# First two projections with K outermost and both token tiles inside, in a hybrid decoder trunk on one core

## The chip, the cores and the metric

One core of one Trainium2 chip. The time is the device time of one execution in microseconds (us). TensorE, VectorE (DVE), ScalarE (ACT), GpSimd (POOL) and SyncE (SP, which issues all transfers here) each run their own queue in order. In the rows PE is TensorE's matmuls and PEld its weight loads.

## What is computed

Two layers on a sequence of 256 tokens and 1024 features, all in float32. Each layer is `x + RMSNorm(mixer(RMSNorm(x)))`; layer 0 is gated linear attention (GLA), layer 1 sparse attention. The change lies in the first projections of layer 0.

```python
def gla_mixer(h, w_in, w_gk_up, b_gk, head_norm, w_out):
    p = (h @ w_in).astype(jnp.float32)
    q, k, v, glr, z = jnp.split(p, [GLA_QK, 2 * GLA_QK, 2 * GLA_QK + GLA_V,
                                    2 * GLA_QK + GLA_V + GLA_GATE_RANK], axis=-1)
    gk = jax.nn.log_sigmoid(glr @ w_gk_up + b_gk) / GLA_GATE_NORMALIZER
    ...
    return o @ w_out
```

## The kernel before

The tokens are two tiles of 128 rows. `h` is x times the norm's gain, transposed so that K (the 1024 features, 8 blocks of 128) lies on the partitions; the row's reciprocal RMS is multiplied in later, when a projection leaves PSUM. Float32 products are kept exact enough by splitting each operand into a rounded high half (`hi`) and the rest (`lo`); a product is three matmuls, hi·hi, and hi·lo and lo·hi (`mm3`, lines 200 to 203). ScalarE writes the high half (a copy that rounds: line 180 for weights, 300 for h); VectorE or POOL subtracts it to get the low half (lines 186 and 301). Which of the two does it is the table `LOS`, one tuple per weight chunk; listed blocks go to POOL.

Weights come in chunks of up to 512 columns (`Chunk`), loaded as four units of two K blocks through four raw buffers (`N_RAW`). A raw buffer is free for the next load when both blocks of its unit are split. All transfers go through one queue on SP in source order (`dma`).

The start of the program, lines 365 to 400: `ch_r` is the first chunk, 352 columns (called r here: the last third of v and the gate's low rank part), then `ch_k` (512 columns, k) and `ch_q` (q). x's first tile comes in two halves of K, its second in one transfer behind all of r's weights. `warm` issues matmuls on a tile of ones. `pre_T` transposes four K blocks of a tile on TensorE, multiplies by the gain (line 297), and splits (300, 301). `proj` (line 212) runs one tile through all eight K blocks, 24 matmuls, then the other tile. `rms` takes two squares with sums on ScalarE (line 315), then VectorE and POOL make the reciprocal root. Rotary angles for layer 1 are made on VectorE (lines 404 to 417: one cast and eight short passes, most on 128x64), their sine and cosine on ScalarE (421 to 424), and behind the cosine ScalarE loads another activation table (428). `spread` (line 320) puts the reciprocal RMS of both tiles on a row with two matmuls (line 329).

What sets the order: the build's scheduler places each engine's instructions, except where `after` or `chain` ties one to the one before it in the source; `act` does so for some of ScalarE's.

Of the kernel before, what the change touches and what calls it, by code (L numbers as in the profile page):

```python
# [23 lines left out]
LOS = ((0, 1, 5, 6, 7), (0, 3, 4, 7), (3, 5, 6), (0, 1, 2, 3, 4, 5, 7), (0, 2, 4, 5, 6), (2, 3, 5, 7), (0, 2, 3, 5, 6), (3, 5, 7), (3, 4, 5, 7), (3, 5, 6), (4, 5, 6, 7), (1, 2, 4, 5, 7), (5, 6), (0, 2, 3, 5), (2, 5, 6), (2, 3, 5, 6, 7), (0, 2, 4, 6), (0, 1, 2, 3, 4, 5, 6, 7), (1, 2, 5))  # L24
# [5 lines left out]
WARM = (7, 1, 7)  # L30
# [57 lines left out]
def hybrid_kernel(ctx: ExitStack, tc: tile.TileContext, x, positions, pre_norm, post_norm,  # L88
# [67 lines left out]
    dma(grow, pre_norm.rearrange("l (k p) -> (l k) p", p=P))  # L156

# [239 lines left out]
    rs0[0], act[0] = rms(0, act[0])  # L397
    for c in range(2):
        act[0] = pre_T(1, c, 0, hT, "s", act[0])
    rs0[1], act[0] = rms(1, act[0])  # L400
# [9 lines left out]
    nc.vector.tensor_scalar(kr, ang, float(1.0 / (2 * np.pi)), MAGIC, op0=ALU.mult, op1=ALU.add)  # L410
    nc.vector.tensor_scalar(kr, kr, MAGIC, None, op0=ALU.subtract)
# [9 lines left out]
    act[0] = after(nc.scalar.activation(SNt[:, :, 1, :], ang, AF.Sin), act[0])  # L421
    nc.scalar.activation(kr, ang, AF.Abs)
    nc.vector.tensor_scalar(kr, kr, -1.0, float(np.pi / 2), op0=ALU.mult, op1=ALU.add)
    sin = nc.scalar.activation(CSt[:, :, 0, :], kr, AF.Sin)
    nc.vector.tensor_scalar(SNt[:, :, 0, :], SNt[:, :, 1, :], -1.0, None, op0=ALU.mult)
    nc.vector.tensor_copy(CSt[:, :, 1, :], CSt[:, :, 0, :])
    with tc.issue_after(sin.ins):
        nc.scalar.preload_act_table_set("natural_log_exp_and_others")
# [7 lines left out]
    ch_k = Chunk(w_in, G_K, 512).load()  # L436
    dma(C1, cst[:, C_L0:C_L1])
# [675 lines left out]
```

## Time and profile before

| | us |
|---|---|
| median of 3 runs (lowest, highest) | 304.49 (303.96, 304.69) |
| profiled execution | 304.3 |
| its span | 302.5 |
| TensorE busy | 285.9 (94%) |
| VectorE, ScalarE, POOL busy | 218.3, 179.2, 164.0 |

The span is the stretch from the first to the last instruction of the profiled execution; its own time lies 1.8 us above it. A busy TensorE means that matmuls were in flight; how dense they were is seen from the distance between their starts. All times in rows are counted from the span's start.

### The profile page before, as it was taken

The page shows a single profiled execution, that of the slowest core. Times are in us where ns is not written, and L with a number is a line of the kernel's source. Part 1 is how long each engine was busy: PE and PEld are TensorE (multiplying, and loading weights), DVE is VectorE, ACT ScalarE, POOL GpSimd, SP SyncE. Part 2 cuts the span into 40 slices and gives each one's busy share as a digit, 9 for nine tenths or more (in the row PEclk, how much of TensorE's full clock was granted, in tenths as well). Part 3 has the DMA queues.
Part 4 walks back from the last instruction along what each step waited for, and adds up shares of the span by engine and source line. Part 5 has one row for each costly group of instructions (what it writes and reads, how often), then busy time and mean ns, then how long its engine had stood idle before and what let it go on. Part 6 is the DMA issues. An engine that isn't in the chain of part 4 may idle for free.

```text
span 302.5 us, 5366 instructions
## 1 busy us (share of the span) xinstructions
PE 285.9 (94%) x1800; PEld 240.1 (79%) x1800; DVE 218.3 (72%) x547; ACT 179.2 (59%) x456; POOL 164.0 (54%) x185
## 2 busy tenths in 40 slices
PE   6998999999999999999979999999899899999991
PEld 6975899999999788777868766899688678677561
DVE  1999628876787758896795544879997999696423
ACT  3697668776595245844533434649896668475311
POOL 2664945898247206473728133598749956424300
PEclk9799999999999999999999999999999999999999
DMA  6976662882847406368583855777404400010001
GB/s 195 314 246 200 185 192 69 275 263 63 307 113 231 144 3 164 117 140 284 149 250 97 259 174 198 272 209 214 136 2 139 142 1 0 2 70 0 2 0 69
DMA packets 28156, 44.56 MB, mean 147 GB/s; under 512 B 2849, under 2 KB 12497, under 8 KB 28130
## 3 DMA queue, kind: packets, MB, share of 16 engines
q1 hardware_dynamic: 28130, 44.23, 47.8%
q8 instruction: 14, 0.23, 0.3%
q14 instruction: 12, 0.10, 0.1%
HBM read 43.18 MB, written 1.05 MB: 146 GB/s over the span
## 4 chain that ended last, share of the span: by engine, by line
PE 54%; DVE 21%; issue 8%; ACT 7%; DMA 6%; POOL 3%; SPq 1%; DVEq 0%; POOLq 0%; ACTq 0%
PE acc L201 10%; PE acc L203 9%; PE acc L202 9%; DVE lo L186 6%; PE o L946 3%; ACT hi L180 3%; PE s L202 3%; PE s L203 3%; PE s L201 3%; PE o L752 3%; DMA raw<-in_gla_w_in_dram 3%; PE s L859 3%; PE t L932 3%; DMA x_sb<-in_x_dram 2%; DMA raw<-in_nsa_w_out_dram 1%
## 5 line engine op out<-in xcount | busy, mean ns | idle before, releaser
L186 POOL TENSOR_TENSOR lo<-raw,hi 128x512 fp32r<-128x512 f32 (+3 forms) x81 | 102.5, 1287 | 58.9 <-ACT hi L180 52.1
L180 ACT ACTIVATE hi<-raw 128x512 fp32r<-128x512 f32 (+3 forms) x152 | 80.3, 580 | 38.4 <-DMA raw<-in_nsa_w_in_dram 23.6
L186 DVE TENSOR_TENSOR lo<-raw,hi 128x512 fp32r<-128x512 f32 (+3 forms) x71 | 61.4, 890 | 17.2 <-ACT hi L180 17.1
L203 PE MATMUL acc<-hi,hT 128*128 128x512 f32 (+3 forms) x128 | 44.6, 349 | 1.0 <-DVE hT L301 1.0
L201 PE MATMUL acc<-hT,hi 128*128 128x256 f32 x160 | 45.3, 284 | 0.1
L203 PE MATMUL acc<-hT,lo 128*128 128x256 f32 x160 | 45.0, 282 | 0.0
L202 PE MATMUL acc<-hT,hi 128*128 128x256 f32 x160 | 44.6, 279 | 0.0
L201 PE MATMUL acc<-hi,hT 128*128 128x512 f32 (+3 forms) x128 | 44.6, 348 | 0.0
L202 PE MATMUL acc<-lo,hT 128*128 128x512 f32 (+3 forms) x128 | 44.2, 346 | 0.0
L903 POOL TENSOR_SCALAR P<-P,cf 128x128 f32<-128x128 f32 (+1 forms) x64 | 30.0, 487 | 26.0 <-DVE cf L899 14.0
L866 ACT ACTIVATE P<-P,mn 128x128 f32<-128x128 f32 (+1 forms) x64 | 28.4, 445 | 9.0 <-DVE mn L864 5.1
L203 PEld LDWEIGHTS acc<-hT,lo 128*128 128x128 f32 x160 | 30.0, 188 | 0.4 <-issue 0.4
L201 PEld LDWEIGHTS acc<-hT,hi 128*128 128x128 f32 x160 | 30.0, 188 | 0.4 <-DVE z L355 0.3
L202 PEld LDWEIGHTS acc<-hT,hi 128*128 128x128 f32 x160 | 30.1, 188 | 0.2
L203 PEld LDWEIGHTS acc<-hi,hT 128*128 128x128 f32 x128 | 24.2, 189 | 4.7 <-DVE hT L301 2.4
L201 PEld LDWEIGHTS acc<-hi,hT 128*128 128x128 f32 x128 | 24.3, 190 | 3.1 <-ACT hi L180 0.4
L202 PEld LDWEIGHTS acc<-lo,hT 128*128 128x128 f32 x128 | 24.4, 190 | 2.1
L864 DVE CUSTOM_DVE_ANT_0 P<-s,c 128x128 f32<-128x128 f32 (+1 forms) x64 | 20.8, 348 | 4.9 <-PE s L859 3.7
L932 PE MATMUL t<-c,P 128*128 128x128 f32 x96 | 16.6, 284 | 0.4 <-DVE qS L827 0.4
L265 POOL TENSOR_TENSOR ss<-ss,cols 128x1 f32<-128x1 f32 x4 | 2.2, 554 | 25.7 <-DVE ss L264 25.7
L932 PEld LDWEIGHTS t<-c,P 128*128 128x128 f32 x96 | 10.6, 141 | 6.2 <-issue 3.8
L690 POOL TENSOR_TENSOR dup<-rt,rt 128x512 f32<-128x512 f32 x6 | 8.6, 1433 | 11.1 <-DVE rt L683 9.0
(235 smaller groups left out, 623.5 us busy)
## 6 DMA issues: line engine op xcount, KB each, us to landing
raw<-in_nsa_w_in_dram SPq DMA_DIRECT2D x24, 512.0 KB, 4.4
raw<-in_gla_w_in_dram SPq DMA_DIRECT2D x16, 512.0 KB, 4.6
raw<-in_gla_w_out_dram SPq DMA_DIRECT2D x8, 512.0 KB, 4.3
raw<-in_nsa_w_out_dram SPq DMA_DIRECT2D x8, 512.0 KB, 4.4
raw<-in_gla_w_in_dram SPq DMA_DIRECT2D x8, 344.0 KB, 3.6
raw<-in_nsa_w_in_dram SPq DMA_DIRECT2D x8, 280.0 KB, 3.2
w<-in_nsa_ck_w_dram SPq DMA_DIRECT2D x4, 512.0 KB, 4.0
w<-in_nsa_cv_w_dram SPq DMA_DIRECT2D x4, 512.0 KB, 4.7
```

The source lines that it names most:

```text
L180: m = after(nc.scalar.activation(hi[:, j, :n], raw[:, j, :n], AF.Copy), prev)
L186: eng.tensor_sub(lo[:, j, :n], raw[:, j, :n], f(hi[:, j, :n]))
L201: m = nc.tensor.matmul(o, a[0], b[0], start=start, stop=False, **kw)
L202: nc.tensor.matmul(o, a[0], b[1], start=False, stop=False, **kw)
L203: return m, nc.tensor.matmul(o, a[1], b[0], start=False, stop=stop, **kw)
L752: nc.tensor.matmul(hid_b[kv * 64:(kv + 1) * 64, :CHID], flat[:, j, kv].rearrange("p g c -> p (g c)"), w1[u * 2 + kv][:, j % 4, :], start=( ...
L859: pe(nc.tensor.matmul(o, q[i], k[:, g, c0:c1], start=(m == 0), stop=(m == 1)))
L864: nc.vector.tensor_tensor_reduce(out=o, in0=src, in1=masks[br], op0=ALU.add, op1=ALU.min, scale=-0.125, scalar=3.0e38, accum_out=self.mn[: ...
L866: nc.scalar.activation(o, o, AF.Exp, scale=-1.0, bias=self.mn[:, j:j + 1], accum_out=self.sm[:, j:j + 1])
L903: nc.gpsimd.tensor_scalar(o, o, cf[:, i * 2 + br:i * 2 + br + 1], 1.0, op0=ALU.mult, op1=ALU.mult)
L932: pe(nc.tensor.transpose(b[:, i * P:(i + 1) * P], self.Pt[i][:, c0:c0 + P], ident))
L946: pe(nc.tensor.matmul(ob[a * 64:(a + 1) * 64, :], (vs_sb, vw_sb)[br][:, kt, g * DH:(g + 1) * DH], pv[:, a], start=(br == y == 0), stop=Fal ...
```

## The change

`ch_r` and `ch_k` no longer go through `proj`. A new function `both` takes one K block and issues six matmuls, the three products for tile 0 and tile 1 in turn, into two PSUM banks; K is the outer loop. h's blocks are made in the order tile 0 first half, tile 1 first half, tile 0 second half, tile 1 second half; the transposes of the second half stand between the matmuls of K blocks 1, 2 and 3. To feed this, x's second tile comes in two halves: its first ahead of r's weights, the second halves of both tiles between the second and the third unit of r's weights. `line` ties the instructions of VectorE, ScalarE and POOL in these steps to source order (`line("dve", ...)` and so on), `in_order` those of TensorE. The squares of tile 0 (`rms(0)`) now stand between the absolute value and the cosine, those of tile 1 between k's first and second unit. The splits of r's low halves are dealt out otherwise (first tuple of `LOS`), and there are 11 instead of 15 warm-up matmuls. The results of r leave PSUM after k's matmuls.

```diff
-LOS = ((0, 1, 5, 6, 7), (0, 3, 4, 7), ...
+LOS = ((0, 2, 3, 5, 6), (0, 3, 4, 7), ...
-WARM = (7, 1, 7)
+WARM = (7, 4)
...
     dma(grow, pre_norm.rearrange("l (k p) -> (l k) p", p=P))
+    dma(X[:, 1, :H], xv[:, 1, :H])
...
-    ch_r = Chunk(w_in, 1712, 352).load(0, 2)
-    dma(X[:, 0, H:], xv[:, 0, H:])
-    ch_r.load(2, 8)
-    dma(X[:, 1, :], xv[:, 1, :])
+    ch_r = Chunk(w_in, 1712, 352).load(0, 4)
+    for t in range(NT):
+        dma(X[:, t, H:], xv[:, t, H:])
+    ch_r.load(4, 8)
...
+    def line(e, ins):
+        queues[e] = after(ins, queues.get(e))
+        return ins
+
+    def in_order(ins):
+        after(ins, last[0])
+        last[0] = ins
...
+    def first_T(t, c):
+        b = bank("ts"[c])
+        for k in range(4):
+            in_order(nc.tensor.transpose(b[:, k * P:(k + 1) * P], X[:, t, (c * 4 + k) * P:(c * 4 + k + 1) * P], ident))
+        xg = base.tile([P, 4, P], F32, tag="xg", name=nm("xg"), bufs=2)
+        def rest():
+            line("dve", nc.vector.tensor_tensor(xg, b.rearrange("p (k n) -> p k n", k=4),
+                                                gT[:, c * 4:c * 4 + 4].unsqueeze(2).to_broadcast([P, 4, P]),
+                                                op=ALU.mult))
+            hi, lo = (a[:, c * 4:c * 4 + 4, t * P:(t + 1) * P] for a in hT)
+            line("act", nc.scalar.activation(hi, xg, AF.Copy))
+            line("dve", nc.vector.tensor_sub(lo, xg, f(hi)))
+        return rest
+
+    def split_in_line(chunk, u):
+        n, raw = chunk.n, chunk.raw[u]
+        hi, lo = (wp.tile([P, 2, 512], F32R, tag=a, name=nm(a), bufs=N_HI) for a in ("hi", "lo"))
+        for j in range(2):
+            line("act", nc.scalar.activation(hi[:, j, :n], raw[:, j, :n], AF.Copy))
+            e, eng = ("pool", nc.gpsimd) if u * 2 + j in chunk.pool else ("dve", nc.vector)
+            line(e, eng.tensor_sub(lo[:, j, :n], raw[:, j, :n], f(hi[:, j, :n])))
+        chunk.u.append((hi, lo))
+
+    def both(o, chunk, k):
+        w = chunk.part(k)
+        for i, j in ((0, 0), (1, 0), (0, 1)):
+            for t in range(NT):
+                m = nc.tensor.matmul(o[t][:, :chunk.n], hT[i][:, k, t * P:(t + 1) * P], w[j], start=(k == i == j == 0),
+                                     stop=(k == KT - 1 and j == 1))
+                in_order(m)
+                chunk.mm.setdefault(2 * k + t, m)
...
-    act[0] = pre_T(0, 0, 0, hT, "t", act[0])
-    act[0] = ch_r.split_unit(act[0])
-    warm(WARM[1])
-    act[0] = pre_T(0, 1, 0, hT, "t", act[0])
-    warm(WARM[2])
-    for u in range(1, 4):
-        act[0] = ch_r.split_unit(act[0])
+    rest.append(first_T(1, 0))
+    for go in rest:
+        go()
+    warm(WARM[1])
+    o_r = [bank("acc") for _ in range(NT)]
+    split_in_line(ch_r, 0)
+    both(o_r, ch_r, 0)
+    split_in_line(ch_r, 1)
+    both(o_r, ch_r, 1)
+    for t in range(NT):
+        first_T(t, 1)()
+        both(o_r, ch_r, 2 + t)
+    for u in (2, 3):
+        split_in_line(ch_r, u)
+        for k in (2 * u, 2 * u + 1):
+            both(o_r, ch_r, k)
...
+    def tables():
+        line("act", nc.scalar.activation(SNt[:, :, 1, :], ang, AF.Sin))
+        line("act", nc.scalar.activation(kr, ang, AF.Abs))
+        nc.vector.tensor_scalar(kr, kr, -1.0, float(np.pi / 2), op0=ALU.mult, op1=ALU.add)
+        rs0[0], queues["act"] = rms(0, queues["act"])
+        sin = line("act", nc.scalar.activation(CSt[:, :, 0, :], kr, AF.Sin))
...
+        with tc.issue_after(sin.ins):
+            queues["act"] = nc.scalar.preload_act_table_set("natural_log_exp_and_others") or sin
+
+    tables()
...
     ch_k = Chunk(w_in, G_K, 512).load()
+    for t in range(NT):
+        if t == 1:
+            rs0[1], queues["act"] = rms(1, queues["act"])
+        split_in_line(ch_k, t)
...
+    o_k = [bank("s") for _ in range(NT)]
+    for u in range(4):
+        if u > 1:
+            split_in_line(ch_k, u)
+        for k in (2 * u, 2 * u + 1):
+            both(o_k, ch_k, k)
```

What this makes of the queues is shown at three places. The first is TensorE where r starts, before: `o` are the warm-up matmuls on `ones`, `t` transposes of x, `acc_240` the bank of tile 0, `hi_117` and `lo_118` the weights of K blocks 0 and 1, `hT_95` and `hT_96` h's high and low half.

```order
L379 MATMUL o_97<-ones 128x128
L292 MATMUL t_124<-c_64,x_sb 128x128 x4
L379 MATMUL o_97<-ones 128x128 x7
L201 MATMUL acc_240<-hi_117,hT_95 128x352
L202 MATMUL acc_240<-lo_118,hT_95 128x352
L203 MATMUL acc_240<-hi_117,hT_96 128x352
```

The same place in the changed program (line numbers are its own; `acc_131` and `acc_132` are the banks of tile 0 and tile 1, `hT_96` and `hT_97` the halves of h):

```order
L395 MATMUL t_115<-c_64,x_sb 128x128 x4
L389 MATMUL o_98<-ones 128x128 x4
L422 MATMUL acc_131<-hi_133,hT_96 128x352
L422 MATMUL acc_132<-hi_133,hT_96 128x352
L422 MATMUL acc_131<-hi_133,hT_97 128x352
L422 MATMUL acc_132<-hi_133,hT_97 128x352
L422 MATMUL acc_131<-lo_134,hT_96 128x352
L422 MATMUL acc_132<-lo_134,hT_96 128x352
```

The two tiles alternate, and the weights' low half is used last of the three.

The second is ScalarE from r's last weights (`hi_152`) to k's first units (`hi_314`, `hi_320`, `hi_326`), before; `junk` are the squares, `hT_95` rounds h of the second tile:

```order
L180 ACTIVATE hi_152<-raw_90 128x352 x2
L315 ACTIVATE junk_159,ss_158<-x_sb 128x512
L315 ACTIVATE junk_161,ss_158<-x_sb 128x512
L300 ACTIVATE hT_95<-xg_173 128x4x128
L180 ACTIVATE hi_314<-raw_221 128x512 x2
L300 ACTIVATE hT_95<-xg_182 128x4x128
L315 ACTIVATE junk_187,ss_186<-x_sb 128x512
L180 ACTIVATE hi_320<-raw_223 128x512 x2
L315 ACTIVATE junk_189,ss_186<-x_sb 128x512
L180 ACTIVATE hi_326<-raw_225 128x512 x2
L421 ACTIVATE sin_t<-ang 128x2x32
L422 ACTIVATE kr<-ang 128x64
```

The same stretch in the changed program (`hi_187`, `hi_205` are r's last two units, `hi_266` and `hi_282` k's first two):

```order
L412 ACTIVATE hi_187<-raw_90 128x352 x2
L412 ACTIVATE hi_205<-raw_92 128x352 x2
L472 ACTIVATE sin_t<-ang 128x2x32
L473 ACTIVATE kr<-ang 128x64
L316 ACTIVATE junk_240,ss_239<-x_sb 128x512
L316 ACTIVATE junk_242,ss_239<-x_sb 128x512
L476 ACTIVATE cos_t<-kr 128x2x32
L480 ACT_TABLE_LOAD
L412 ACTIVATE hi_266<-raw_258 128x512 x2
L316 ACTIVATE junk_273,ss_272<-x_sb 128x512
L316 ACTIVATE junk_275,ss_272<-x_sb 128x512
L412 ACTIVATE hi_282<-raw_260 128x512 x2
```

The sine, the cosine and the table load moved ahead of k's first unit; the squares of tile 0 moved behind the sine.

The third is VectorE in the same stretch, before: `lo_141` and `lo_147` are low halves of r's weights, `xg` products of the second tile, `ang` and `kr` the angles.

```order
L186 TENSOR_TENSOR lo_141<-raw_86,hi_140 128x352 x2
L186 TENSOR_TENSOR lo_147<-raw_88,hi_146 128x352
L404 CAST cols<-posi 128x2
L408 TENSOR_SCALAR ang<-c_64,cols 128x32 x2
L297 TENSOR_TENSOR xg_173<-s_168,gT 128x512
L410 TENSOR_SCALAR kr<-ang 128x64
L297 TENSOR_TENSOR xg_182<-s_177,gT 128x512
L411 TENSOR_SCALAR kr<-kr 128x64
L316 TENSOR_TENSOR ss_158<-ss_158 128x1
L301 TENSOR_TENSOR hT_96<-xg_173,hT_95 128x4x128
```

In the changed program (`xg_162` and `xg_177` are the second halves of K of tile 0 and 1, `lo_188` and `lo_206` the low halves of r's last units that fall to VectorE):

```order
L399 TENSOR_TENSOR xg_162<-s_157,gT 128x512
L404 TENSOR_TENSOR hT_97<-xg_162,hT_96 128x4x128
L399 TENSOR_TENSOR xg_177<-s_172,gT 128x512
L404 TENSOR_TENSOR hT_97<-xg_177,hT_96 128x4x128
L414 TENSOR_TENSOR lo_188<-raw_90,hi_187 128x352
L414 TENSOR_TENSOR lo_206<-raw_92,hi_205 128x352
L455 CAST cols<-posi 128x2
L457 TENSOR_SCALAR ang<-c_64,cols 128x32 x2
L459 TENSOR_SCALAR kr<-ang 128x64
L460 TENSOR_SCALAR kr<-kr 128x64
L465 SCALAR_TENSOR_TENSOR ang<-kr,ang 128x64 x3
L466 TENSOR_SCALAR ang<-ang 128x64
```

The angle passes, which stood in among the products, now stand together behind r's last low half.

## Rows read from the trace of the kernel before

**Rows 1.** The page, part 1: busy us, share of the span, instructions.

```profile
PE 285.9 (94%) x1800; PEld 240.1 (79%) x1800; DVE 218.3 (72%) x547; ACT 179.2 (59%) x456; POOL 164.0 (54%) x185
```

**Rows 2.** Windows by stage: us, busy by engine (instructions), granted clock, DMA share, GB/s.

```profile
0.00:10.14 10.14, 7.61 (x39) 7.16 (x40) 3.15 (x6) 4.24 (x8) 3.27 (x14) 0.90 0.77 245
10.14:20.68 10.54, 9.81 (x58) 9.19 (x58) 10.50 (x22) 8.53 (x22) 6.51 (x6) 0.94 0.88 277
20.68:34.12 13.44, 12.03 (x53) 9.07 (x51) 12.93 (x23) 10.20 (x19) 8.88 (x8) 1.00 0.64 184
34.12:46.13 12.01, 12.01 (x102) 11.91 (x100) 3.95 (x8) 7.43 (x14) 7.29 (x8) 1.00 0.64 183
```

**Rows 3.** Waits of TensorE, 0 to 34: total us, times, longest.

```profile
PE acc L203 <- DVE hT L301: 0.7, 2, 0.5
```

**Rows 4.** Waits of TensorE, 34.12 to the end, the two longest.

```profile
PE o L752 <- DVE flat L743: 1.6, 1, 1.6
PE acc L201 <- DVE z L355: 1.3, 1, 1.3
```

**Rows 5.** Timeline of TensorE: start, us, instruction, count, [idle before <- what ended it].

```profile
7.17 0.65 PE L292 MATMUL t<-c,x_sb 128*128 128x128 f32 x4 [1.25 <-DMA x_sb<-in_x_dram]
...
10.14 0.64 PE L201 MATMUL acc<-hi,hT 128*128 128x352 f32 x1
...
12.44 1.04 PE L292 MATMUL s<-c,x_sb 128*128 128x128 f32 x8
...
13.64 0.33 PE L201 MATMUL acc<-hi,hT 128*128 128x352 f32 x1
...
15.56 0.33 PE L201 MATMUL acc<-hi,hT 128*128 128x352 f32 x1
...
26.66 0.50 PE L202 MATMUL s<-lo,hT 128*128 128x512 f32 x1 [1.32 <-DVE lo L186]
...
27.46 0.76 PE L329 MATMUL t<-dg,onesr 128*128 128x256 f32 x2
28.05 0.40 PE L202 MATMUL s<-lo,hT 128*128 128x512 f32 x1
...
33.89 0.40 PE L203 MATMUL s<-hi,hT 128*128 128x512 f32 x1
```

**Rows 6.** Timeline of ScalarE, 6 to 31.

```profile
6.13 0.63 ACT L300 ACTIVATE hT<-xg 128x512 fp32r<-128x512 f32 x1 [4.13 <-DVE xg L297]
6.67 0.87 ACT L180 ACTIVATE hi<-raw 128x352 fp32r<-128x352 f32 x2
...
11.44 0.61 ACT L315 ACTIVATE junk<-x_sb 128x512 f32<-128x512 f32 x1
...
12.18 0.63 ACT L315 ACTIVATE junk<-x_sb 128x512 f32<-128x512 f32 x1
...
20.17 0.24 ACT L421 ACTIVATE sin_t<-ang 128x64 f32<-128x64 f32 x1
...
25.70 1.28 ACT L428 ACT_TABLE_LOAD   x1
...
27.43 3.23 ACT L180 ACTIVATE hi<-raw 128x512 fp32r<-128x512 f32 x6
```

**Rows 7.** Timeline of VectorE, 16 to 19.

```profile
16.12 0.21 DVE L416 SCALAR_TENSOR_TENSOR ang<-kr,ang 128x64 f32<-128x64 f32 x1
...
16.37 1.20 DVE L416 SCALAR_TENSOR_TENSOR ang<-kr,ang 128x64 f32<-128x64 f32 x1
...
18.24 0.68 DVE L301 TENSOR_TENSOR hT<-xg,hT 128x512 fp32r<-128x512 f32 x1
```

**Rows 8.** Timeline of POOL: two low halves of r, one of k.

```profile
7.23 1.82 POOL L186 TENSOR_TENSOR lo<-raw,hi 128x352 fp32r<-128x352 f32 x2 [5.25 <-ACT hi L180]
...
22.34 1.29 POOL L186 TENSOR_TENSOR lo<-raw,hi 128x512 fp32r<-128x512 f32 x1
```

**Rows 9.** Windows, 8 to 12, columns as in rows 2.

```profile
8.00:12.00 4.00, 4.00 (x21) 4.00 (x20) 4.00 (x6) 3.42 (x9) 2.21 (x4) 0.57 1.03 346
```

More of the change, by code (lines that the diff above doesn't have):

```diff
@@ L372, in hybrid_kernel @@
     hT = new_hT()
-    act = [None]
     wb = bank("o")
+    queues = {}
+    def line(e, ins):
[4 more added lines that the diff above has]
+        last[0] = ins
     def warm(n):
         for _ in range(n):
-            m = nc.tensor.matmul(wb[:, :P], ones, ones, start=True, stop=True)
-            after(m, last[0])
-            last[0] = m
+            in_order(nc.tensor.matmul(wb[:, :P], ones, ones, start=True, stop=True))
@@ L383, in hybrid_kernel @@
     warm(WARM[0])
-    nc.tensor.transpose(wb[:, P:P + 2 * KT], grow, ident[:2 * KT, :2 * KT])
+    rest = [first_T(0, 0)]
+    in_order(nc.tensor.transpose(wb[:, P:P + 2 * KT], grow, ident[:2 * KT, :2 * KT]))
     gT = base.tile([P, 2 * KT], F32, tag="gT", name="gT")
-    nc.vector.tensor_copy(gT, wb[:, P:P + 2 * KT])
-    act[0] = pre_T(0, 0, 0, hT, "t", act[0])
-    act[0] = ch_r.split_unit(act[0])
+    line("dve", nc.vector.tensor_copy(gT, wb[:, P:P + 2 * KT]))
+    rest.append(first_T(1, 0))
@@ L396, in hybrid_kernel @@
     rs0 = [None, None]
[L397 to L400, printed above, removed]
     HD = DH // 2
-    nc.vector.tensor_copy(pos, posi)
     ang = base.tile([P, NT, HD], F32, tag="ang", name="ang")
     kr = base.tile([P, NT, HD], F32, tag="kr", name="kr")
+    line("dve", nc.vector.tensor_copy(pos, posi))
     for t in range(NT):
-        nc.vector.tensor_scalar(ang[:, t, :], cc("inv"), pos[:, t:t + 1], None, op0=ALU.mult)
+        line("dve", nc.vector.tensor_scalar(ang[:, t, :], cc("inv"), pos[:, t:t + 1], None, op0=ALU.mult))
@@ L409, in hybrid_kernel @@
     MAGIC = 12582912.0
[L410 to L411 removed]
+    line("dve", nc.vector.tensor_scalar(kr, ang, float(1.0 / (2 * np.pi)), MAGIC, op0=ALU.mult, op1=ALU.add))
+    line("dve", nc.vector.tensor_scalar(kr, kr, MAGIC, None, op0=ALU.subtract))
     c1 = 6.28125
@@ L415, in hybrid_kernel @@
     for cw in (c1, c2, c3):
-        nc.vector.scalar_tensor_tensor(ang, kr, -cw, ang, op0=ALU.mult, op1=ALU.add)
-    nc.vector.tensor_scalar(ang, ang, 3.1415925, -3.1415925, op0=ALU.min, op1=ALU.max)
+        line("dve", nc.vector.scalar_tensor_tensor(ang, kr, -cw, ang, op0=ALU.mult, op1=ALU.add))
+    line("dve", nc.vector.tensor_scalar(ang, ang, 3.1415925, -3.1415925, op0=ALU.min, op1=ALU.max))
     CSt = base.tile([P, NT, 2, HD], F32, tag="cos", name="cos_t")
     SNt = base.tile([P, NT, 2, HD], F32, tag="sin", name="sin_t")
[L421 to L428, printed above, removed]
+    def tables():
[4 more added lines that the diff above has]
+        sin = line("act", nc.scalar.activation(CSt[:, :, 0, :], kr, AF.Sin))
+        nc.vector.tensor_scalar(SNt[:, :, 0, :], SNt[:, :, 1, :], -1.0, None, op0=ALU.mult)
+        nc.vector.tensor_copy(CSt[:, :, 1, :], CSt[:, :, 0, :])
+        with tc.issue_after(sin.ins):
+            queues["act"] = nc.scalar.preload_act_table_set("natural_log_exp_and_others") or sin
+    tables()
     wraw = lp.tile([32, 512], F32, tag="E", name="wraw")
@@ L506, in hybrid_kernel @@
     ch_q = Chunk(w_in, G_Q, 512).load()
-    simple(ch_k, lambda o, t: nc.scalar.activation(ksb[:, t, :], o, AF.Copy, scale=rs0[t]), None, "s")
+    for t in range(NT):
+        nc.scalar.activation(ksb[:, t, :], o_k[t], AF.Copy, scale=rs0[t])
     ch_v0 = Chunk(w_in, 1024, 344).load()
```

12 lines of the change are left out of this document (6 added, 6 removed).

## The prediction

> **What bounds the kernel now.** Read the engines' busy times first: TensorE is busy 94% of the span [rows 1]. Then the stages, cut where TensorE passes from one projection to the next [rows 2]: the first projection r (352 columns) starts at 10.14 and lasts 10.54 us, the second, k (512 columns), lasts 13.44, the third, q, starts at 34.12 and is busy throughout. From there TensorE hardly waits again: the longest waits are 1.6 and 1.3 us, both for VectorE work that is itself fed by earlier matmuls [rows 4]. So what moves the start of q moves the end by the same amount, as long as the queues behind q are as before. They are: on all five engines the order of both programs is the same row by row once q's gate transposes are past, some four microseconds after q has started. I carry the shift in full. If the two long waits took some of it up, at most 2.9 us of a delay would go; I take nothing, since both follow TensorE's own results.
>
> What the first two stages should cost: matmuls of r at full clock start 0.16 us apart (12 steps from 13.64 to 15.56), those of k 0.234 (25 steps from 28.05 to 33.89) [rows 5]. With 48 each that is 7.7 and 11.2 us. r loses 2.8: eight transposes from 12.44 on (0.8 us), two waits for the second tile's low halves of h (0.7) [rows 3], the rest a slow start at half clock. k loses 2.2: one wait of 1.32 before 26.66, some pipeline around it, and the two matmuls of `spread`, which push the next one from 27.46 to 28.05, 0.59 us [rows 5]. So 12 us of stages 2 and 3 lie on TensorE and 5 are to be had at most; the change can win some, if nothing else makes TensorE wait.
>
> **Start of r.** VectorE's queue is now fixed as product, low half, product, low half for the first K half of the two tiles. The first product comes as before, and ScalarE rounds it from 6.13, 0.63 long [rows 6]. Then follow the low half 0.68 [rows 7], the second tile's product, a pass of the same 512 columns, so 0.68 again, and its rounding from 8.1. ScalarE's next instruction starts 0.54 after a rounding's start (6.13 to 6.67), now the first of r's weights, and that takes 0.48 (two in 0.87, the second 0.39 after the first): first matmul at 9.1 instead of 10.14. The data is there: before, the fifth transfer ended TensorE's wait at 7.17 [rows 5]; now the weights' first unit is the fifth, with the same bytes ahead of it. Gain: **1.0 us**. All of x's second tile and the weights land under this work, so the moved transfers cost nothing; if the second tile's half came only at 7.2 as the fifth did, it would still be ahead of its product at 7.4.
>
> **Middle of r.** Twelve matmuls for k=0,1 take 1.9 us at full clock; with POOL's first low half (0.91, from two in 1.82 [rows 8]) they end near 11.4. At half clock, as the trace has it for most of 8 to 12 [rows 9], they end up to 1.2 later. Now the second half of K hangs on one chain, in line on VectorE and ScalarE: four transposes 0.44 (half of the eight from 12.44 [rows 5]), product 0.68, rounding 0.63, low half 0.68, product of the other tile 0.68, rounding 0.63: 15.2 to 16.4. ScalarE's next weights stand behind it (four, 0.39 apart), so k=4 starts at 15.7 to 16.9. TensorE has finished k=2 and 3 by 14.3 to 15.5 and waits 1.4. Then 24 matmuls, 3.9 us, and a little for POOL's low halves: r ends between 19.8 and 21.0, centre **20.4**, against 20.68. What was gained at the start is mostly spent here.
>
> **Between r and k.** This is the term that decides. Before, ScalarE rounded k's first units at 15 to 20 us, in among the squares and the second tile, and its sine, cosine and table load came later, where TensorE had work. Now, as the order shows, ScalarE's queue after r's last weights reads sine, absolute value, two squares, cosine, table load, and only then k's first unit. The sine waits for the angle chain on VectorE, nine small dependent passes that stand behind r's last low half. Step by step: r's last rounding ends 16.8 to 18.0; VectorE's last low half 0.5 to 1.0 later, centre 18.2; the chain at 0.21 each with nothing beside it (row of 16.12) is 1.8, between 1.2, if the passes overlap as the trace's short ones do, and 2.6, if one is held as the same pass at 16.37 was, 1.20 beside POOL's work [rows 7]. POOL has nothing queued ahead of rstd there, so I take 1.8: 20.0. Sine and absolute value, 0.24 each and overlapping, 0.4; two squares 0.74 each (11.44 to 12.18), 1.5; cosine, as the sine, 0.25; table load 1.28; first rounding of k 0.6 (six in 3.23) [rows 6]. Sum: 20.0+0.4+1.5+0.25+1.28+0.6 = **24.0** for k's first matmul; the ends of all terms give 22.6 and 25.6. TensorE is idle from 20.4 to 24.0, which the old order did not have. Before, the table load ran from 25.70, beside the 1.32 us in which TensorE waited for VectorE's low half anyway; that cover is gone.
>
> **k and q.** k's matmuls are 11.2. The first low half is POOL's, 1.29 long or more [rows 8], against 0.94 of matmuls that may run before it: 0.45 of waiting. ScalarE's two squares of the second tile stand ahead of the second unit, but TensorE needs 2.8 us per unit and ScalarE 1.5 and 1.1: no wait. `spread` now stands behind k, 0.59. Together 12.2 us against 13.44: **1.2 us** won. q starts at 24.0+12.2 = 36.2, against 34.12: **2.1 us later**, 0.8 to 3.7 by the ends. The weights of q come later too, since their buffers are freed by k's low halves, but q needs its last unit only 8 us in; ScalarE's decay chain for the gates slips by about the same two microseconds, so nothing overtakes TensorE.
>
> **The clock.** TensorE's granted clock fell to half (1.2 of 2.4 GHz) at 8 us, after it had been idle 1.25 us before 7.17 [rows 5, 9]. It did not fall after the wait of 1.32 before 26.66, in the middle of dense matmuls: stage 3 has 1.00 [rows 2]. A standstill of 3.6 us is between two and three times either of these, so I take it that the clock falls. What it costs is read from the stretch that the trace has: a mean of 0.57 over 8 to 12 is 3.4 us at half clock [rows 9]. That is 1.7 us of lost work if it lies fully in k's matmuls, 0.8 if half of it lies in the standstill. I take **1.4**, with 0 and 2.5 as ends (nothing, or a stretch and a half).
>
> The Trainium skill, page "TensorE: Matmul & The Clock Gate", section "Loop structure matters more than you think", says that a nest in which the matmuls come in dense groups keeps the clock up and that one which waits between groups lets it drop to half. By that rule the later start would be 3.5 us in all; by the row of 26.66 alone it would be 2.1. The trace bears out both sides, one fall and one that did not come.
>
> **Sum.** Start -1.0, r's chain and ScalarE's queue together +4.3, so that k starts 3.3 later, k -1.2, clock +1.4: **+3.5 us**. Against the profiled execution's 304.3 this is 307.8; the median of the runs is 304.49, 0.2 above it, and the prediction is for that: 308.0.
>
> **Rivals.** *The clock stays.* For it speaks the 1.32 us wait without a fall. Then +2.1: 306.6, or 305.4 to 306.8. Chance 0.17. *ScalarE's detour is short.* If VectorE's small passes overlap and the clock stays, k starts at 22.6 and the time is within 0.3% (0.9 us, about what this kernel's runs can tell from no change): 0.10. *Faster.* ScalarE's idle time is covered: the angle passes slip in early and k's first rounded weights are ready when r ends. Place: the first matmul of k; before 21.9 (34.12 less 12.2) the change wins, at 20.4 it wins 1.5 us, 303.0. Against it stands the fixed order of both queues; for it, that VectorE's share in the stretch is inferred, and that both stages are dense where nothing waits. Chance 0.11. *Two stretches of half clock*, or half clock in r's second half too, since TensorE waits there 1.4 us as well: 310 or more, 0.10. That the change would not do what it says is out: the order shows the new rows.
>
> **How the numbers follow.** The forecast (306.8 to 309.0, likeliest 308.0) has 0.52. The range 304.9 to 309.7 takes in the clock rival and most of the ends, and leaves out the faster case, half of the middle one and the far end of the slowest. Slower by over 0.3%: 0.52+0.17+0.10 = 0.79; within 0.3%: 0.10; faster: 0.11.
>
> **What would show it.** In the profile after: first matmul of r near 9.1; a wait of TensorE of 1 to 1.5 us before k=4 of r, released by ScalarE; the table load on ScalarE at about 22, and right behind it the rounding that ends a TensorE standstill of 3 to 4 us; granted clock 0.5 for some 3 us inside k; q's first matmul between 36 and 38; every stage after it as long as before. Wrong would be: k's first matmul before 22, the clock at 1.00 throughout k, or a later stage that gives the shift back.

## The result and the profile after

The changed kernel takes 311.32 us (median of 4 runs, 311.22 to 312.71) where the kernel before takes 304.34: a ratio of 1.024, 95% interval 1.0208 to 1.0272, 7 us slower. The profiled execution takes 311.22, its span is 309.4, 6.9 longer than before. The forecast was 308.0 with a range up to 309.7: the sign was right, the size too small by half.

The page's first part has hardly changed against [rows 1]; all engines do the same work:

```profile
PE 286.5 (93%) x1792; PEld 239.5 (77%) x1792; DVE 217.7 (70%) x547; ACT 179.3 (58%) x456; POOL 165.3 (53%) x185
```

The windows by stage, cut at the same events as [rows 2] (start, first matmul of r, end of its last, first of k, of q, and of the gates' `t<-ct,gk`, which before stands at 46.13); the last row is the stretch at half clock inside k. Columns: us, busy time by engine (instructions), granted clock, DMA share, GB/s.

```profile
0.00:9.46 9.46, 5.97 (x31) 5.35 (x31) 2.56 (x5) 2.98 (x5) 1.45 (x12) 1.00 0.77 248
9.46:20.73 11.27, 9.58 (x56) 8.41 (x56) 7.47 (x16) 3.93 (x9) 5.45 (x5) 1.00 0.53 154
20.73:24.98 4.25, 0.00 (x1) 0.00 (x0) 1.03 (x7) 3.85 (x10) 0.56 (x1) 1.00 0.72 241
24.98:40.41 15.43, 14.33 (x50) 11.08 (x51) 13.70 (x20) 11.23 (x23) 12.48 (x10) 0.78 0.55 160
40.41:52.84 12.43, 12.06 (x102) 11.77 (x101) 4.47 (x9) 8.66 (x17) 6.86 (x8) 1.00 0.67 200
25.95:32.78 6.83, 5.74 (x14) 4.26 (x14) 5.71 (x8) 5.94 (x14) 6.48 (x5) 0.50 0.51 148
```

r begins 0.7 earlier and ends where it did. Then TensorE stands still for 4.25 us, and k, which was to become shorter, becomes 2.0 longer, 6.83 us of it at a granted clock of 0.50 (1.2 of 2.4 GHz). From the first `t<-ct,gk` to the end it is 256.6 us, against 256.4 before: nothing behind the first 53 us gives anything back or takes more.

The standstill in TensorE's timeline (start, us, instruction, count, [idle before <- what ended it]), to be set against [rows 5]:

```profile
16.41 0.91 PE L422 MATMUL acc<-hi,hT 128*128 128x352 f32 x4 [1.45 <-ACT hi L412]
...
24.98 1.28 PE L422 MATMUL s<-hi,hT 128*128 128x512 f32 x4 [4.25 <-ACT hi L412]
27.36 1.22 PE L422 MATMUL s<-lo,hT 128*128 128x512 f32 x2 [1.09 <-POOL lo L414]
```

and ScalarE in the same stretch, against [rows 6]:

```profile
21.07 0.26 ACT L472 ACTIVATE sin_t<-ang 128x64 f32<-128x64 f32 x1 [3.55 <-DVE ang L466]
...
21.38 0.61 ACT L316 ACTIVATE junk<-x_sb 128x512 f32<-128x512 f32 x1
...
22.12 0.63 ACT L316 ACTIVATE junk<-x_sb 128x512 f32<-128x512 f32 x1
...
22.75 0.24 ACT L476 ACTIVATE cos_t<-kr 128x64 f32<-128x64 f32 x1
23.01 1.28 ACT L480 ACT_TABLE_LOAD   x1
24.30 1.15 ACT L412 ACTIVATE hi<-raw 128x512 fp32r<-128x512 f32 x2
```

This is the queue the prediction described: ScalarE itself idles 3.55 us with k's first rounding in its queue, because the sine at the head waits for VectorE's angles (k's first two units had landed: in the kernel with the detour put late, below, ScalarE rounds them by 19.62 without a wait); then it works through squares, cosine and table load while TensorE waits.

### The profile page after: what moved, and what is told of

Its sections match the earlier page's. It is cut to its first block, busy times and chain, and to the rows that moved or that the text cites. A ratio compares the mean times of both kernels' runs of the same rounds, so it can differ in the third digit from the quotient of the medians.

```text
span 309.4 us, 5355 instructions
## 1 busy us (share of the span) xinstructions
PE 286.5 (93%) x1792; PEld 239.5 (77%) x1792; DVE 217.7 (70%) x547; ACT 179.3 (58%) x456; POOL 165.3 (53%) x185
## 4 chain that ended last, share of the span: by engine, by line
PE 58%; DVE 17%; issue 9%; ACT 5%; DMA 5%; POOL 4%; SPq 1%; POOLq 0%; DVEq 0%; ACTq 0%
PE acc L202 11%; PE acc L204 10%; PE acc L203 10%; DVE lo L187 4%; DMA raw<-in_gla_w_in_dram 4%; PE o L1012 3%; PE s L204 3%; PE s L203 3%; PE s L202 3%; PE o L818 3%; PE s L925 3%; PE t L998 3%; ACT hi L181 2%; DMA raw<-in_nsa_w_out_dram 2%; DVE flat L809 1%
## 5 line engine op out<-in xcount | busy, mean ns | idle before, releaser
L187 POOL TENSOR_TENSOR lo<-raw,hi 128x512 fp32r<-128x512 f32 (+2 forms) x72 | 92.0, 1298 | 47.7 <-ACT hi L181 47.4
L181 ACT ACTIVATE hi<-raw 128x512 fp32r<-128x512 f32 (+2 forms) x136 | 72.5, 584 | 38.0 <-DMA raw<-in_nsa_w_in_dram 21.5
L187 DVE TENSOR_TENSOR lo<-raw,hi 128x512 fp32r<-128x512 f32 (+2 forms) x64 | 56.4, 903 | 16.9 <-ACT hi L181 16.8
L204 PE MATMUL acc<-hi,hT 128*128 128x512 f32 (+2 forms) x112 | 39.1, 349 | 0.3 <-DVE hT L302 0.3
L202 PE MATMUL acc<-hi,hT 128*128 128x512 f32 (+2 forms) x112 | 39.0, 349 | 0.0
L203 PE MATMUL acc<-lo,hT 128*128 128x512 f32 (+2 forms) x112 | 38.9, 347 | 0.0
L204 PEld LDWEIGHTS acc<-hi,hT 128*128 128x128 f32 x112 | 21.0, 188 | 3.4 <-DVE hT L302 1.1
L202 PEld LDWEIGHTS acc<-hi,hT 128*128 128x128 f32 x112 | 21.1, 188 | 3.1 <-ACT hi L181 0.4
L203 PEld LDWEIGHTS acc<-lo,hT 128*128 128x128 f32 x112 | 21.1, 189 | 2.0
L414 POOL TENSOR_TENSOR lo<-raw,hi 128x352 fp32r<-128x352 f32 (+1 forms) x9 | 11.4, 1293 | 11.7 <-ACT hi L412 11.7
L998 PEld LDWEIGHTS t<-c,P 128*128 128x128 f32 x96 | 10.6, 140 | 6.2 <-issue 3.9
```

Source lines behind the costliest of these rows:

```text
L181: m = after(nc.scalar.activation(hi[:, j, :n], raw[:, j, :n], AF.Copy), prev)
L187: eng.tensor_sub(lo[:, j, :n], raw[:, j, :n], f(hi[:, j, :n]))
L202: m = nc.tensor.matmul(o, a[0], b[0], start=start, stop=False, **kw)
L203: nc.tensor.matmul(o, a[0], b[1], start=False, stop=False, **kw)
L204: return m, nc.tensor.matmul(o, a[1], b[0], start=False, stop=stop, **kw)
L414: line(e, eng.tensor_sub(lo[:, j, :n], raw[:, j, :n], f(hi[:, j, :n])))
```

## The experiments

The question was whether ScalarE's detour (sine to table load ahead of k's first unit) is the cause, or the nest itself, or the clock; and then why mending the detour does not mend the time. In each kernel the stages are read by three starts: k's first matmul, q's, and the first `t<-ct,gk`.

**The nest: k one tile after the other.** Everything else as in the changed kernel.

```diff
-    for u in range(4):
-        ...
-            both(o_k, ch_k, k)
+    for t in range(NT):
+        for k in range(KT):
+            w = ch_k.part(k)
+            for i, j in ((0, 0), (1, 0), (0, 1)):
+                m = nc.tensor.matmul(o_k[t], hT[i][:, k, t * P:(t + 1) * P], w[j], ...)
```

> The changed kernel with k's matmuls alone put back to one tile after the other, 24 and 24; r and all queues as changed. Theory: the standstill and the half clock stay as they are, so the time is 311.3 within 1 us. Rival (alternating two banks and two stationary tiles costs TensorE time): k's matmuls come closer together than 0.234 us at full clock and the time falls to 310 or less.

311.96 us, ratio 1.0197 (1.0151 to 1.0244); k from 25.0, the same standstill of 4.3, q at 40.51. At full clock k's matmuls still start 0.23 us apart (three from 37.01 to 37.71). k's nest is not the cause of the standstill or of the time.

**The detour put later, the build's scheduler left free behind it.**

```diff
-    tables()
...
-    for t in range(NT):
-        if t == 1:
-            rs0[1], queues["act"] = rms(1, queues["act"])
-        split_in_line(ch_k, t)
+    for u in range(2):
+        split_in_line(ch_k, u)
+    tables()
+    rs0[1], queues["act"] = rms(1, queues["act"])
```

> The changed kernel with sine, cosine, table load and the squares of both tiles moved on ScalarE behind k's second unit; nothing else is edited, the build places POOL's work anew. Theory (ScalarE's detour between r and k, and the half clock that follows from the standstill, are the whole loss): k's first rounded weights are ready by 18.5 us, k starts at r's end near 20.7 instead of 24.98, the clock stays at 1.00, k takes 11.2 plus at most 1, q starts near 33 instead of 40.4, and the time is 303.5 to 305. Rival (the nest with K outermost or the moved transfers cost time of their own): q starts no earlier than 37 and the time stays at 308 or more.

315.31 us, ratio 1.0311 (1.0255 to 1.0367). The standstill is gone (k at 20.29), q comes at 36.98, 3.4 earlier than in the changed kernel, and still the time is longer: the scheduler placed the rest anew, with waits of 2.7 and 3.1 us at 86 and 110 us, where the changed kernel waits not at all and 0.3. The run tells nothing of the detour's price; what it taught is that all other rows have to be tied.

**No order fixed at all for VectorE, ScalarE and POOL** (`line` ties nothing; TensorE's order stays).

```diff
     def line(e, ins):
-        queues[e] = after(ins, queues.get(e))
         return ins
```

> The changed kernel with K outermost, both tiles inside and the new transfers, but VectorE's, ScalarE's and POOL's queues left to the build's scheduler instead of source order. The scheduler puts all of k's roundings ahead of sine, cosine and table load, and r's last units ahead of the second half of K. Theory (only the fixed order costs): no standstill of over 1 us between r and k, clock 1.00, time 303 to 305. Rival (the nest or the transfers cost): 308 or more.

309.61 us, ratio 1.0113 (1.0057 to 1.0169). The expected 303 to 305 did not come, because the scheduler's order has waits of its own. r now lasts from 8.39 to 28.2, with waits of 3.3 and 1.1 us for the low and high half of h and a mean granted clock of 0.83. k, whose weights are all rounded by then, is dense (28.23 to 39.65, 11.42 us at clock 1.00). So k loses nothing by its nest when its weights are there.

**Both orders made well.** The same source, transfers and TensorE order as the changed kernel; the rows of ScalarE, VectorE and POOL are put in an order worked out from the durations and releases of this kernel's traces, and every row of the four engines is then tied to the one ahead of it. ScalarE between r's weights and q's, changed kernel (-) and this one (+), the units of k in words:

```diff
 hi (r, last unit)
-sine, abs, 2 squares, cosine, table load, k unit 0, 2 squares, k units 1 to 3, wup
+square, k unit 0 (first block), square, wup, k unit 0 (second), 2 squares, k units 1, 2 (first blocks),
+abs, sine, k units 1, 2 (second blocks), cosine, k unit 3 (first), table load, k unit 3 (second)
```

> The changed kernel with the same matmuls in the same order on TensorE and the same transfers, but another fixed order of ScalarE, VectorE and POOL in the first 75 us: all of r's and k's roundings stand where their data lands, the squares fill ScalarE's gaps, sine, cosine and table load stand among k's last units, the low halves of k ahead of small work that nobody waits for, the gates' casts ahead of the next weights' low halves. Theory (the loss is only the order of the queues): r ends near 18 to 19, no standstill of TensorE ahead of k, clock 1.00 in k, k 11.2 to 12.2, first matmul of q at 30 to 32, 2 to 4 us ahead of the kernel before, 300.0 to 302.5. Rival (K as the outer loop, or x in halves, costs time by itself): q not ahead of 36, 306 or more.

**The same, with the detour put back:** sine, absolute value, two squares, cosine and table load ahead of k's first unit, VectorE's angle passes with them; nothing else moves.

```diff
 hi (r, last unit)
+sine, abs, 2 squares, cosine, table load
-square, k unit 0 (first block), square, wup, k unit 0 (second), 2 squares, ...
+k unit 0 (first block), wup, k unit 0 (second), 2 squares, ...
```

> e5 with one thing put back: on ScalarE sine, absolute value, the two squares of tile 0, cosine and table load stand again ahead of k's first rounding, and the passes of VectorE that feed them ahead of its first low half of k. All else as in e5. Theory: a standstill of 3 to 4 us ahead of k, clock at half for two stretches (6.83 us) that start within it or 1 us behind it, 1.5 to 2.9 us lost to that; e5 plus 5.5 to 7.5. Rival (a second chain, of late weights, is nearly as late, so the detour matters little): e5 plus less than 3.

The first took 300.73 us, ratio 0.988 (0.9861 to 0.9899): 1.2% faster than the kernel before, and faster than every other one here. The second took 306.91, ratio 1.0079 (1.0059 to 1.0099). The windows of the first (k, then q's stage) and of the second (k, q's stage, and the stretch at half clock):

```profile
18.33:29.75 11.42, 11.42 (x52) 9.25 (x51) 11.17 (x28) 9.88 (x21) 6.49 (x7) 1.00 0.86 243
29.75:41.77 12.02, 12.02 (x103) 11.93 (x102) 6.32 (x10) 10.31 (x22) 11.15 (x12) 1.00 0.69 197
```

```profile
22.63:36.24 13.61, 13.44 (x50) 10.31 (x51) 11.62 (x21) 10.29 (x22) 10.39 (x10) 0.87 0.58 159
36.24:48.33 12.09, 12.09 (x101) 12.00 (x101) 6.90 (x10) 9.67 (x21) 10.10 (x10) 1.00 0.63 179
23.55:26.96 3.41, 3.37 (x9) 2.38 (x8) 2.44 (x8) 3.38 (x9) 2.77 (x5) 0.50 0.38 101
```

and the row at which the second kernel's k starts:

```profile
22.63 1.33 PE L529 MATMUL s<-hi,hT 128*128 128x512 f32 x4 [3.26 <-ACT hi L519]
```

Without the detour k runs 11.4 us with no gap, directly behind r. With it, k starts 4.3 later behind a standstill of 3.26 and takes 2.2 longer, at half clock for 3.41 us. Of the 4.3, 0.85 was there at r's first matmul (8.96 against 8.11), where both kernels still have the same rows: in that execution the first four matmuls of r took 1.33 us, in the other 0.90. By the medians of all runs the detour alone costs **6.2 us**; the changed kernel stands 10.6 above the good order, so the other 4.4 lie in its other rows.

**The detour with the clock held up.** 14 matmuls on the tile of ones, whose result is used nowhere, fill the standstill of the kernel with the detour; r's last matmul stands behind them.

```diff
+    warm(14)        # behind r
```

> e7 with 14 matmuls on the tile of ones between r and k, some 3.0 us, so that TensorE does not stand still. Theory: clock 1.00 in k, k starts when it does in e7; e7 less 1.5 to 2.9, the price of the clock where no second chain is near. Rival (what e2 seemed to show, that the clock costs next to nothing in the end): within 0.6 of e7.

307.41 us, ratio 1.0087 (1.0066 to 1.0109), the same as without them. TensorE's timeline:

```profile
22.05 1.19 PE L529 MATMUL s<-hi,hT 128*128 128x512 f32 x4 [0.16 <-ACT hi L519]
...
35.68 0.36 PE L309 MATMUL acc<-hT,hi 128*128 128x256 f32 x1 [1.44 <-DVE v L612]
```

The clock stays at 1.00. k begins 0.6 earlier, but so does r (8.38 against 8.96), so that is not the fill. k's last matmul of all comes 1.9 earlier than without the fill, 1.3 of it by the clock. Then q waits 1.44 us for `v`: VectorE's read of r's result out of the banks that q is to write. Without and with the fill:

```profile
35.54 1.03 DVE L611 SCALAR_TENSOR_TENSOR v<-acc,rs_r,v 128x336 fp32r<-128x336 f32 x2
```

```profile
34.98 1.03 DVE L612 SCALAR_TENSOR_TENSOR v<-acc,rs_r,v 128x336 fp32r<-128x336 f32 x2
```

In both kernels q starts 0.7 us after the start of this row (36.24 and 35.68): the read is earlier by the 0.6 of r's start and by nothing else. The half clock was real and cost nothing at the end here, because VectorE's chain was as late.

**The changed kernel with the clock held up**, first with the scheduler free, then with all rows tied as in the changed kernel (there r's last matmul stands behind the 18).

```diff
+    warm(18)        # behind r
```

> The changed kernel with 18 more matmuls on ones between r and k, which keep TensorE at work through the standstill; ScalarE's queue is as it was. Theory: k's first matmul still comes at about 25, the granted clock stays at 1.00, k takes 12.4 instead of 15.2 us, and the time falls by 2.9 to about 308.4. Rival (k is slow because the low halves come late, and the clock only accompanies it): k still takes 15 us and the time stays at 311.3.

> The changed kernel with 18 matmuls on the tile of ones between r and k, as in e2, but with ScalarE, VectorE, POOL and TensorE tied row by row to the orders that the changed kernel has (in e2 two rounding passes of ScalarE and one low half had moved). This is the clock alone. Theory 1 (the half clock lies on the path to the end): clock 1.00 in k, q 1.7 to 2.9 earlier, 308.4 to 309.6. Theory 2 (a second chain is nearly as late: k's split is late, so q's and v's weights are loaded late, and VectorE's cast of the gates stands behind the low half of v's last unit): clock 1.00, q earlier by as much, but a new wait of 1.5 to 2.5 us ahead of the gates' matmul on wup, and 310.5 to 311.8.

**The changed kernel with the detour behind k's second unit, all other rows tied** (the standstill without its cause, and VectorE and ScalarE otherwise as they were); then also the second of the gates' two casts (`glrT`), for which TensorE had waited, ahead of VectorE's next low half; then also the seven low halves of k and q that are POOL's given to VectorE.

```diff
 hi (r, last unit)
+k units 0, 1
 sine, abs, 2 squares, cosine, table load
-k unit 0
 2 squares
-k unit 1
```

> The changed kernel with sine, absolute value, the squares, cosine and table load behind k's second unit on ScalarE (as in e1), the small passes of VectorE and POOL that hang on them behind k's first low halves, and every other row tied to the order of the changed kernel (in e1 much behind had moved). Theory 1 (ScalarE's queue is the one cause, what follows shifts with TensorE): no standstill, q at 36 to 37, ct at 48.5 to 49.5, 307 to 308. Theory 2 (the weights behind k are late by themselves, since four buffers feed everything): q at 36 to 37 too, then a wait of 2 to 3.5 ahead of the gates' matmul, and 309.5 to 311.5.

> e10 with one row more moved: VectorE's two casts of the gates stand ahead of the low half of v's last unit. Theory 2: the wait ahead of the gates' matmul goes, ct starts 2 to 3 us earlier than in e10, and some of it comes back at the next late result: e10 less 0.3 to 2. Theory 1: no wait was there, so within 0.5 of e10.

> e11 with one thing changed: the seven low halves of k and q that POOL makes are made by VectorE, each beside its neighbour of the same unit, in the same order; all else as in e11. In e11 TensorE waits 2.0 us ahead of q for VectorE's read of r's results, and VectorE's low halves there take 1.3 to 1.8 us beside a POOL pass and 0.68 without one. Theory 2 sharpened (VectorE and POOL exclude each other on passes between SBUF tiles, so POOL's low halves cost VectorE more than they take off it): though VectorE gets 7 passes of 0.6 more, its read of r's results comes earlier, the waits of 0.7 and 0.6 in k go, q starts at 33.5 to 35.5 against 37.65, ct at 47 to 49.5 against 51.98, e11 less 2 to 4.5. Rival (VectorE is simply full there, POOL took work off it): VectorE ends 4 us later, q at 39 or later, e11 or more.

| kernel | us | ratio (95%) | k | q | `t<-ct,gk` |
|---|---|---|---|---|---|
| changed | 311.32 | 1.024 (1.0208, 1.0272) | 24.98 | 40.41 | 52.84 |
| + 18 matmuls, free | 312.73 | 1.0227 (1.018, 1.0275) | 25.01 | 38.69 | 51.77 |
| + 18 matmuls, tied | 312.05 | 1.0262 (1.0238, 1.0287) | 24.62 | 39.96 | 53.52 |
| detour late | 312.29 | 1.0253 (1.0227, 1.0279) | 20.58 | 37.86 | 52.42 |
| and casts early | 310.58 | 1.0227 (1.0197, 1.0256) | 20.38 | 37.65 | 51.98 |
| and POOL's low halves moved | 311.25 | 1.0219 (1.0198, 1.024) | 20.35 | 34.47 | 48.02 |

Up to 4.6 us are won at k's start and up to 5.9 at q's, and none of it arrives: all stay within 1.5 us of the changed kernel. (The last three columns come from the profiled execution; that of the last three kernels took 310.46, 310.16 and 309.28, each below its median.) In the last kernel q and the gates start where they were expected, but the time, expected 2 to 4.5 us below that of the kernel ahead, is 0.7 above it. What takes over is in TensorE's waits up to 58 us. The changed kernel (waited for, us in total, times, longest):

```profile
PE s L422 <- ACT hi L412: 4.3, 1, 4.3
...
PE s L422 <- POOL lo L414: 1.1, 1, 1.1
...
PE t L554 <- DVE glrT L549: 0.4, 1, 0.4
```

With 18 matmuls, tied:

```profile
PE s L523 <- POOL lo L515: 2.0, 1, 2.0
PE t L656 <- DVE glrT L651: 1.3, 1, 1.3
```

With the detour late:

```profile
PE acc L303 <- DVE v L605: 2.0, 1, 2.0
PE s L523 <- ACT hi L513: 1.1, 1, 1.1
...
PE s L523 <- DVE lo L515: 0.8, 1, 0.8
PE s L523 <- POOL lo L515: 0.6, 1, 0.6
PE t L655 <- DVE glrT L650: 0.5, 1, 0.5
```

With the detour late, casts early and POOL's low halves moved:

```profile
PE t L698 <- DVE tmp L661: 2.1, 1, 2.1
PE acc L303 <- DVE v L605: 1.5, 2, 0.7
```

The 4.3 us for ScalarE turn, by turns, into waits for POOL's low half, for the gates' casts, for `v` and for the gates' decay (`tmp`). With 18 matmuls and the scheduler free the clock stays at 1.00 and q starts 1.7 earlier; a wait of 2.12 for `tmp` at 54.67 takes that back. With all rows tied a wait of 1.99 brings half clock back (28.32 to 31.73), so there the matmuls did not keep it away, and the two with the detour late have half clock too, from 37.82 and 38.73 on, about the wait for `v`. The last kernel has none and starts the gates 4.8 us earlier than the changed kernel; then it waits 2.06 at 50.73, and of its lead 1.9 is left at the end of the profiled span (307.5). That execution lies 2 us below the median of its runs; what the other executions gave back no trace shows. That wait leads back to the transfers: between 34 and 52 us ScalarE, whose roundings stand ahead of the gates' decay in its queue, waited (us in total, times, longest)

```profile
ACT hi L282 <- DMA raw<-in_gla_w_in_dram: 3.0, 3, 1.2
```

three times for weights to land; the last of these waits ended at 43.14, and the decay's first pass followed at 43.92.

A kernel that is the changed one with all rows tied and nothing else was not run; these four rest on the tying costing nothing.

**The nest's own worth.** The kernel before, with its nest and transfers, its rows put in order and tied in the same way.

> The kernel before, its matmuls and transfers as they are, with ScalarE, VectorE and POOL ordered for the first 75 us in the same way as in e5. Theory: the order of the queues was also before not the best one; k's waits (1.3 us) and the two waits in r (0.7) go, q starts at 31.5 to 33, 301.5 to 303.5; what K as the outer loop is worth by itself is then e6 less e5, 0.5 to 2 us. Rival (the order before was tuned as far as it goes): within 0.9 of 304.3.

302.51 us, ratio 0.993 (0.9906 to 0.9955): k from 20.09, dense (11.43 us), q at 31.52. Against the same done to the changed kernel (300.73) K outermost and x by halves are worth 1.8 us, nearly all of it in k's earlier start (18.33); neither order is known to be the best for its nest, so 1.8 is a comparison of two good ones.

## Why the prediction was right or wrong, step by step

| | before | predicted | after |
|---|---|---|---|
| first matmul of r | 10.14 | 9.1 | 9.46 |
| wait before k=4 | | 1.4 | 1.45 |
| end of r | 20.68 | 20.4 | 20.73 |
| first matmul of k | 20.68 | 24.0 | 24.98 |
| start of q | 34.12 | 37.6 | 40.41 |
| end of the span | 302.5 | 306.0 | 309.4 |

The sign and the path were right. What failed is the size of three terms on that path, the largest the clock: 1.4 us was taken, 2.9 measured. The angle chain was taken at 1.8 and took 2.7, and the wait for POOL's first low half was taken at 0.45 and took 1.09.

- **r** came within 0.4 us of what was worked out, with the right releaser: what the start wins, h's second half spends. Of the 0.36 by which the start was late, 0.27 lie in the first product, which was to come as before and came at 5.68 instead of 5.41.
- **Between r and k: right mechanism, 1.0 too short.** VectorE's last low half of r ends at 18.33 (18.2 predicted). Then the chain of angles took 2.7 us where I took 1.8, and all that follows took 3.9 where the sum says 4.0. Most of the excess, 0.7, is its first row, beside POOL's low halves of r:

```profile
16.83 2.30 POOL L414 TENSOR_TENSOR lo<-raw,hi 128x352 fp32r<-128x352 f32 x2 [4.19 <-ACT hi L412]
...
18.25 0.91 DVE L455 CAST cols<-posi 128x2 f32<-128x2 int32 x1
...
20.85 0.19 DVE L466 TENSOR_SCALAR ang<-ang 128x64 f32<-128x64 f32 x1
```

  A cast of two columns ended at 19.16; POOL's low halves of r ran from 16.83 to 19.13. "POOL has nothing queued ahead of rstd there" was the false sentence. The row that warned, the 1.20 us pass beside POOL's work [rows 7], had been kept for the far end of the range, and the cast itself had been as long before, beside POOL's low halves from 10.84 to 13.95. In the kernel with the detour, where POOL is idle from 13.29 to 15.79, it takes 0.16. Before, and in the kernel with the detour:

```profile
12.18 0.90 DVE L404 CAST cols<-posi 128x2 f32<-128x2 int32 x1
```

```profile
15.58 0.16 DVE L562 CAST cols<-posi 128x2 f32<-128x2 int32 x1
```

- **k's matmuls: 0.6 too short.** POOL's first low half was to make TensorE wait 0.45; it was 1.09. POOL's timeline shows why: POOL first cast a constant, for whose transfer it had waited, and then took 1.77 for the low half, beside one of VectorE's, where 1.29 was taken.

```profile
25.08 0.50 POOL L518 CAST ct<-c 128x384 fp32r<-128x384 f32 x1 [1.22 <-DMA c<-in_cst_dram]
25.54 1.77 POOL L414 TENSOR_TENSOR lo<-raw,hi 128x512 fp32r<-128x512 f32 x1
```

- **The clock: 1.5 too short.** That it would fall was right, its length was not: 6.83 us against the 3.4 of [rows 9], twice the stretch, which was the fourth rival (310 or more, at 0.10). With 11.2 of matmuls and 1.09 of waiting, k's 15.2 us up to `spread` leave 2.9 for it; 1.4 was taken. The fall came 0.97 us after the burst began, behind 4.25 us of idleness; a second wait lies inside the stretch, and in the kernel with the detour, where that wait is missing, the stretch is 3.41. Whether that wait is what doubled it was not tried.
- These three make 3.1 of the 3.4 that the sum lacked. `spread` gave 0.36 back (0.23 from its first matmul to q's, against 0.59); q's stage is 0.4 longer (12.43 against 12.01, with a wait of 0.37 for `glrT`), and the rest 0.2. (The low end of q's shift, given as 0.8, is 0.7 by its own terms; nothing hangs on it.)
- **"Nothing overtakes TensorE" was the deeper mistake**, though it hardly shows in the sum. I followed the one chain that ended last and priced its pieces as if each could be had or saved by itself. The runs show several chains about equally late: with the changed kernel's other rows kept, TensorE's standstill could be taken away without any gain at the end, and in the good order with the detour so could the half clock. VectorE is the first of the others. In the changed kernel it works without a gap from 28.63 to 42.42, and its second read of r's result ends at 39.95, 0.5 before q starts in that bank:

```profile
28.63 1.31 DVE L326 TENSOR_SCALAR dg<-c,rs_r 128x128 f32<-128x128 f32 x1 [0.45 <-POOL rs_r L251]
29.86 3.47 DVE L414 TENSOR_TENSOR lo<-raw,hi 128x512 fp32r<-128x512 f32 x2
...
39.40 0.55 DVE L504 SCALAR_TENSOR_TENSOR v<-acc,rs_r,v 128x336 fp32r<-128x336 f32 x1
```

  The rows before showed it: in stage 3 VectorE is busy 12.93 of 13.44 us [rows 2], more than TensorE. I read that row for TensorE alone. The next are the weights on their way through four raw buffers to ScalarE, and the gates' decay behind them: the 2.06 us wait of the last kernel.
- **Later stages:** carried in full, as predicted (256.6 against 256.4 us).

The cause is shown as far as this: the same nest and TensorE order run 1.2% faster or 0.8% slower than before by the place of the detour alone, and 2.4% slower with the rest of the changed kernel's rows. Which of those other rows carry the 4.4 us was not separated.

## What to carry to other kernels

When an order is written out by hand, look in each in-order queue for an instruction that waits for another engine and stands ahead of the work that feeds TensorE: here one sine that waited 3.55 us (3.01 in the good order), with squares and a table load behind it, turned a nest that was worth 1.8 us into a loss of 2.4 (306.91 against 304.51); the loss of 7 took the changed kernel's other rows too. Before pricing a wait or a half clock, read the busy time of every engine in that stage: here VectorE was busy for 12.93 of 13.44 us before and had no gap from 28.63 to 42.42 after, and taking TensorE's wait away moved nothing at the end. And compare two nests only with the order of all engines good for each; the order was worth more here (10.6 us) than the nest.

## What the runs showed of the hardware

**VectorE and POOL hold each other up.** A low half of 128x512 takes VectorE 0.68 us with POOL idle, the next starting 0.60 after it, and up to 1.78 beside POOL's low halves; POOL's takes 1.29 [rows 8] and, behind VectorE's, up to 1.77. In the last of the kernels above, with POOL's low halves moved, VectorE's timeline reads

```profile
20.74 2.49 DVE L515 TENSOR_TENSOR lo<-raw,hi 128x512 fp32r<-128x512 f32 x4
...
27.84 2.90 DVE L515 TENSOR_TENSOR lo<-raw,hi 128x512 fp32r<-128x512 f32 x4
```

four in 2.5 us with POOL idle, and four in 2.9 with one POOL cast (29.25 to 30.19) beside them. In the changed kernel the row of 29.86 has two in 3.47, beside POOL's three:

```profile
28.57 4.22 POOL L414 TENSOR_TENSOR lo<-raw,hi 128x512 fp32r<-128x512 f32 x3
```

Dealing such work out to both engines gained nothing in this stage: from k's first matmul to q's VectorE was busy 10.61 us (29 instructions) without POOL's help, and 13.35 (30) with it in the kernel ahead, and q came 3.2 us earlier (the time at the end did not: 311.25 against 310.58). The Trainium skill, page "SBUF — State Buffer", section "Who interferes with whom", calls the port pair that the two share an exclusive lock, which a VectorE instruction with two SBUF inputs contends for with a GpSimd instruction that reads SBUF. The trace agrees for the low halves, and `v`, which reads PSUM, is not held (0.55 at 39.40, beside POOL's low halves from 37.63 to 40.63; 0.56 at 33.76 in the last kernel, with POOL idle). By the same section of the Trainium skill a VectorE instruction with one SBUF input contends only in a two-port mode; the cast of 0.91 and the 1.31 us `dg` at 28.63, which have one each, were long beside POOL's work too, and which mode they ran in no row tells. The last two kernels show the same on equal rows: the two `ang` passes behind the cast took 2.48 us beside POOL's low halves and 0.39 with these moved, `dg` 1.30 and 0.29.

**TensorE's clock.** Standstills of 4.25 and 3.26 us were followed by half clock, for 6.83 and 3.41 us, about 1 us after matmuls ran again. Waits near 2 us went either way: 1.99, 2.00 and 2.01 with a fall, of 3.4 us each, 2.06, 2.12 and, ahead of r in the changed kernel, 2.25 without one, as the two of 1.44 and 1.45; before, 1.25 came with one [rows 5, 9]. So the length of a wait alone did not tell it here. The Trainium skill, page "TensorE: Matmul & The Clock Gate", section "Loop structure matters more than you think", on which the prediction weighed the fall, is borne out in that the standstill brought it. What no row on TensorE could show is that the lost clock cost nothing at the end of the kernel with the detour (306.91 us with it, 307.41 without).
